# A list schedule that knows of the port between VectorE and GpSimd, and a fused alpha·x + bias

## The chip, the core and the metric

The kernel runs on one core of a Trainium2 chip. The metric is device microseconds of one execution; before the change the median of 3 runs is 1795.09 us (1792.98 to 1796.85). The engines' names in the profile: PE is TensorE (PEld its weight loads), DVE VectorE, ACT ScalarE, POOL GpSimd, SP the engine that issues the DMAs.

## What is computed

One inference step of a two-layer encoder (`DEPTH = 2`, width 1024), for 512 rows of a prompt and, beside it, 128 rows of samples (8 streams of 16 frames, with a cache of 1024 past frames each). Everything is fp32. Cut to what matters:

```python
for l in range(DEPTH):
    p = x @ w_in[l]
    y = [rms(y_A) | rms(y_B) | rms(y_C)] * g_mix[l]   # gMLP gating, latent attention, stick-breaking attention
    x = layer_norm(ALPHA * x + y @ w_out[l], ln1_g[l], ln1_b[l])
    h = square(relu(x @ w_up[l] + b_up[l])) @ w_down[l] + b_down[l]
    x = layer_norm(ALPHA * x + h, ln2_g[l], ln2_b[l])
```

The last line holds the term that the change touches: `ALPHA * x + b_down` is formed ahead, and the product with `w_down` is added to it.

## The kernel before

**Two lanes.** The prompt (`p_layer`, tiles t = 1 to 4 of 128 rows) and the samples (`s_layer`, tile t = 0) are two generators. `weave` lets them issue their instructions in turn. All rows live in one SBUF tile `xy` of 128 x 5 x 1024.

**fp32 by halves.** A matmul takes operands of a rounded type. So each fp32 operand is split in two: ScalarE copies it into the rounded type (`hi`), and then another engine subtracts that from the source (`lo`). Three matmuls (`mm3`, hi·hi, hi·lo, lo·hi) make one product. `split` (L577) does this; its subtraction goes to VectorE, except where the caller names GpSimd. VectorE does it for the weights (tiles w, wx, wS), for the hidden layer (hT) and for transposed activations out of PSUM (yT, pTs and others); GpSimd does it for the cached keys and values (cT, cN) and their rotary part (kr). The weights' and the cache's raw data, rawP, rawS, rawK and rawV, come by DMA into small rings.

**The stretch around the change, prompt.** `p_out_mlp` (L895) multiplies y with `w_out` in two halves of 512 columns, tile by tile. After the second half of tile t it calls `layer_norm` (L628): two bn_stats and a bn_aggr on VectorE give mv; `rstd_of` (L596) makes rs out of it in two instructions on GpSimd, a tensor_scalar and a power; two scalar_tensor_tensor on VectorE apply it, the first with mv and the gain, the second with rs and the bias. Gain, bias and `b_down` lie in tiles named hT, as they take slots of the ring that the hidden layer uses later. Then comes `x1(t - 1)` (L915): 8 transposes on TensorE of the tile before, with their splits, and in place on GpSimd the multiplication by ALPHA and the addition of `b_down`. The result is read again when the products with `w_down` are added, after the first four blocks of the hidden layer (`dve.tensor_tensor(xy, xy, pa, ADD)`, 128x512).

**The same for the samples.** `s_out_mlp` (L1686) does it for tile 0 alone (its two GpSimd instructions are L1715 and L1716); gain and bias lie in the ring rawS.

**What sets the order.** The generators do not issue into the engines' queues in their own order. Each instruction is noted in a `Plan` (`note`, L161) with its engine, a cost (`cost_of`, L365) and its dependencies. When all is noted, `ranks` gives each instruction a rank and `schedule` (L208) makes one list: it keeps a time at which each engine is free (`free`), takes the engine that can start first, and on it the instruction of the lowest rank among those that are ready by then. `issue` (L285) sets the instruction's start and end. `follow` (L358) fixes each engine's resulting order in the program, with no wait of its own: an instruction on the chip starts when its engine has come to it and its data are there. An instruction's `kind` is "copy" for `dve.tensor_copy` and empty otherwise; a "copy" starts when GpSimd is free, and GpSimd is free when it has ended. No `dve.tensor_copy` is called in the kernel. Nothing else in the list connects VectorE's time with GpSimd's. All instructions are issued by the helper at L403, so that the profile names them by tiles and not by lines.

Of the kernel before, what the change touches and what calls it, by code (L numbers as in the profile page):

```python
# [96 lines left out]
class Plan:  # L97

    AFTER = dict(pe=0.17, act=0.0, dve=0.0, pool=0.0, sp=0.0)
    HOP = dict(pe=0.055, act=0.035, dve=0.035, pool=0.08, sp=0.03)
    LAP = dict(pe=0.0, act=0.1, dve=0.08, pool=0.0, sp=0.0)

# [53 lines left out]
            self.masks[key] = r  # L158
        return self.masks[key]

    def note(self, eng, cost, ins, outs, srcs, kind="", nbytes=0):  # L161
        k = len(self.ops)
        deps = set()
        for ap, w in [(x, False) for x in srcs] + [(x, True) for x in outs]:
            t = self.tiles.get(ap.tensor.name)
            if t is None:
                continue
            m = self.region(ap)
            t["ops"].add(k)
            deps.update(o for o, x in t["writes"] if x & m)  # L170
            if t["tag"]["pool"]["psum"]:
                deps.add(t["bank"].get(eng, k))
                t["bank"][eng] = k
            if w:
                deps.update(o for o, x in t["reads"] if x & m or (t["tag"]["pool"]["psum"] and eng == "pe"))
                t["reads"] = [(o, x) for o, x in t["reads"] if x & ~m]
                t["writes"] = [(o, x) for o, x in t["writes"] if x & ~m] + [(k, m)]
            else:
                t["reads"].append((k, m))
        deps.discard(k)  # L180
        self.ops.append(dict(eng=eng, cost=cost, ins=ins, deps=deps, kind=kind, bytes=nbytes, then=[], by=self.now["by"], phase=self.now[self.now["by"]]))
        return k

    def glue(self, k0):
# [23 lines left out]
    def schedule(self, prio):  # L208
# [38 lines left out]
        end = [0.0] * n  # L247
        ready = [0.0] * n
        free = dict(pe=0.0, act=0.0, dve=0.0, pool=0.0, sp=0.0)
        dma = 0.0  # L250
        later = {e: [] for e in free}
        able = {e: [] for e in free}
        order = {e: [] for e in free}
# [29 lines left out]
                grant(t)  # L283

        def issue(k, e, s):  # L285
            nonlocal dma
            o = ops[k]
            if o["kind"] == "copy":
                s = max(s, free["pool"])
            if e == "sp":  # L290
                free[e] = s + 0.42
                dma = max(dma, s + 1.3) + o["bytes"] / 320e3
                f = dma + 0.45
            else:
                free[e] = s + o["cost"] - self.LAP[e]
                f = s + o["cost"] + self.AFTER[e]
                if o["kind"] == "copy":
                    free["pool"] = max(free["pool"], f)
            end[k] = f
            o["at"] = s  # L300
            order[e].append(k)
            for name in o["tiles"]:
                left[name] -= 1
                if not left[name]:
                    t = self.tiles[name]["tag"]
                    last = max(end[x] + 0.05 for x in self.tiles[name]["ops"])
                    t["slots"].append(last)
                    t["slots"].sort()
                    for x in opens.get(name, ()):
                        block[x] -= 1  # L310
                        floor[x] = max(floor.get(x, 0.0), last)
                        if not block[x]:
                            grant(self.tiles[x]["tag"])
                    grant(t)
            for x in succ[k]:
                hop = 0.0 if ops[x]["eng"] == e == "pe" else f + self.HOP[ops[x]["eng"]]
                ready[x] = max(ready[x], hop)
                need[x] -= 1
                if not need[x] and x not in glued:
                    loose(x)  # L320
# [7 lines left out]
        while done < n:  # L328
            best = None
            for e in free:  # L330
                if able[e]:
                    s = free[e]
                elif later[e]:
                    s = max(free[e], later[e][0][0])
                else:
                    continue
                if best is None or s < best[0]:
                    best = s, e
            if best is None:
                raise RuntimeError(f"no order: {n - done} left")  # L340
            s, e = best
            while later[e] and later[e][0][0] <= s:
                r, p, k = heapq.heappop(later[e])
                heapq.heappush(able[e], (p, k))
            p, k = heapq.heappop(able[e])
            while True:
                issue(k, e, s)
                done += 1
                if not ops[k]["then"] and not run:
                    break  # L350
                run = ops[k]["then"] + run
                k = run.pop(0)
                s = max(free[e], ready[k])
# [31 lines left out]
class Timed:  # L385
# [5 lines left out]
    def __getattr__(self, name):  # L391
        f = getattr(self.eng, name)

        def call(out, *a, **k):
            if name.startswith("preload"):
                r = f(out)
                self.pace.plan.note(self.key, 1.3, r.ins, [], [])
                return r
            ins = [x for n, x in [*enumerate(a), *k.items()] if isinstance(x, bass.AP) and n != "accum_out"]
            outs = [out] + ([k["accum_out"]] if "accum_out" in k else [])  # L400
            cost = cost_of(self.key, name, out, ins, "accum_out" in k)
            self.pace.add(self.key, cost, out.tensor.name, [x.tensor.name for x in ins])
            r = f(out, *a, **k)  # L403
            kind = "copy" if self.key == "dve" and name == "tensor_copy" else ""
            self.pace.plan.note(self.key, cost, r.ins, outs, ins, kind)
            return r
        return call


class Loads:  # L410
# [5 lines left out]
    def dma_start(self, out, src):  # L416
        self.pace.load(out.tensor.name, src.tensor.name, 4 * math.prod(out.shape))
        r = self.eng.dma_start(out, src)
        self.pace.plan.note("sp", 0.42, r.ins, [out], [src], "", 4 * math.prod(out.shape))
        return r  # L420


# [61 lines left out]
def hybrid_step(  # L484
# [410 lines left out]
    def p_out_mlp(l):  # L895
# [18 lines left out]

        def x1(t):  # L915
            transpose_x(xy[:, t], XT[:, 0, :, cols(t)], XT[:, 1, :, cols(t)], "acc")
            pool.tensor_scalar(xy[:, t], xy[:, t], ALPHA, 0.0, ALU.mult, ALU.add)
            pool.tensor_tensor(xy[:, t], xy[:, t], bd, ALU.add)

        l1 = 0.0  # L920
        for c in range(2):
# [764 lines left out]
    def s_out_mlp(l):  # L1686
# [25 lines left out]
        xT = so.tile([128, 2, 8, 128], F32R, tag="xS", name="x1TS")  # L1712
        yield at("sC", pace.t)
        transpose_x(xy[:, 0], xT[:, 0], xT[:, 1], "sC")
        pool.tensor_scalar(xy[:, 0], xy[:, 0], ALPHA, 0.0, ALU.mult, ALU.add)  # L1715
        pool.tensor_tensor(xy[:, 0], xy[:, 0], bcast(b_down[l], D), ALU.add)  # L1716
        yield at("x")
        down = [bank("x") for _ in range(2)]
        hts = []
# [47 lines left out]

    weave(nc, pace, thread(p_layer), thread(s_layer), RATE, now)
    order = pace.plan.schedule(pace.plan.ranks(*SPAN))
    print("PLAN span", pace.plan.span, "pe idle", pace.plan.idle)  # L1770
    pace.plan.follow(tc, order)


# [97 lines left out]
```

## Time and profile before

| what | value |
|---|---|
| median of 3 runs | 1795.09 us |
| the profiled execution, its own time | 1795.59 us |
| its span, first to last instruction | 1793.8 us |
| TensorE busy | 1683.3 us (94%) |
| VectorE busy | 1181.2 us (66%) |
| ScalarE busy | 994.7 us (55%) |
| GpSimd busy | 584.8 us (33%) |
| DMA queue of the loads and stores | 303.49 MB, 52.8% of 16 engines |
| granted TensorE clock, mean | 0.984 |

The first line is the kernel's time; the second is the one execution that the profile shows. The span leaves out what lies ahead of the first and after the last instruction. Busy time is the sum of an engine's instructions, with whatever each of them waited for after it had begun; a share is over the whole span, in which stretches with different limits follow each other. What the rows below show of waits is the idle time of an engine ahead of an instruction, put down to the engine and the tile that ended it.

### The profile page before, as it was taken

What the parts mean: (1) busy time and instruction counts of PE and PEld (TensorE: products, weight loads), DVE (VectorE), ACT (ScalarE), POOL (GpSimd) and SP (SyncE); (2) the same over time, 40 slices, a digit from 0 to 9 for tenths busy, and PEclk for the clock granted to TensorE, in tenths of its full rate; (3) what the DMA queues carried; (4) which work ended last, traced back from release to release, by engine and by line L of the source; (5) the groups of instructions that cost most, each with busy time, mean ns of one, the idle gap of its engine ahead of it and who ended that gap; (6) DMA issues with size and microseconds to landing.
All of it is one profiled execution on the core that took longest, in us unless ns stands there. A gap on an engine that the chain in (4) does not pass through costs nothing.

```text
span 1793.8 us, 24450 instructions
## 1 busy us (share of the span) xinstructions
PE 1683.3 (94%) x8756; PEld 1408.1 (78%) x8756; DVE 1181.2 (66%) x1582; ACT 994.7 (55%) x1739; POOL 584.8 (33%) x498
## 2 busy tenths in 40 slices
PE   8998999899999999999899989898999899999998
PEld 6888888677777778888688878787777677788886
DVE  3586685856676587666726766768566765876766
ACT  4575784545656556563226747745457555564631
POOL 0123455844564310000101324568446542100001
PEclk9999999999999999999999999999999999999999
DMA  6225566346445687674452356553465446875732
GB/s 248 92 70 169 192 173 213 117 141 203 152 134 160 178 280 239 199 249 130 151 154 71 101 156 192 173 196 118 151 201 156 139 143 190 269 245 187 254 127 91
DMA packets 145818, 305.06 MB, mean 170 GB/s; under 512 B 32032, under 2 KB 46496, under 8 KB 145696
## 3 DMA queue, kind: packets, MB, share of 16 engines
q1 hardware_dynamic: 145696, 303.49, 52.8%
q8 instruction: 69, 1.13, 0.3%
q14 instruction: 53, 0.43, 0.1%
HBM read 286.14 MB, written 17.30 MB: 169 GB/s over the span
## 4 chain that ended last, share of the span: by engine, by line
PE 56%; DVE 12%; DMA 10%; ACT 8%; POOL 7%; issue 6%; SPq 1%; POOLq 0%; ACTq 0%; DVEq 0%
PE acc L403 38%; PE sC L403 9%; PE x L403 8%; POOL rs L403 2%; POOL cN L403 2%; DVE xy L403 2%; DMA rawV<-in_t_ckvv_dram 2%; DVE a L403 2%; POOL cT L403 2%; DMA rawK<-in_t_ckv_dram 1%; DVE wx L403 1%; DMA rawP<-in_w_down_dram 1%; ACT w L403 1%; DVE z L403 1%; DVE w L403 1%
## 5 line engine op out<-in xcount | busy, mean ns | idle before, releaser
L403 PE MATMUL acc<-w,hT 128*128 128x512 f32 x1536 | 397.9, 397 | 4.1 <-ACT hT L403 3.6
L403 PE MATMUL acc<-yT,wx 128*128 128x512 f32 (+1 forms) x1632 | 399.2, 387 | 1.6 <-DVE wx L403 0.8
L403 PEld LDWEIGHTS acc<-yT,wx 128*128 128x128 f32 x1632 | 292.5, 191 | 59.7 <-DVE wx L403 1.7
L403 PEld LDWEIGHTS acc<-w,hT 128*128 128x128 f32 x1536 | 281.3, 188 | 66.5 <-ACT hT L403 6.0
L403 POOL TENSOR_TENSOR cT<-rawK,cT 128x512 fp32r<-128x512 f32 x128 | 187.9, 1475 | 192.5 <-ACT cT L403 167.3
L403 POOL TENSOR_TENSOR cN<-rawV,cN 128x512 fp32r<-128x512 f32 x128 | 189.8, 1488 | 154.1 <-ACT cN L403 152.3
L403 DVE TENSOR_TENSOR w<-rawP,w 128x1024 fp32r<-128x1024 f32 (+4 forms) x122 | 152.8, 1256 | 126.2 <-ACT w L403 124.4
L403 DVE TENSOR_TENSOR wS<-rawS,wS 128x1024 fp32r<-128x1024 f32 x144 | 179.2, 1249 | 81.2 <-ACT wS L403 80.4
L403 ACT CAST wS<-rawS 128x1024 fp32r<-128x1024 f32 x144 | 150.9, 1050 | 132.1 <-PE x L403 64.6
L403 PE MATMUL acc<-w,xT 128*128 128x512 f32 (+3 forms) x960 | 189.4, 353 | 5.1 <-DVE ev L403 2.5
L403 POOL TENSOR_SCALAR rs<-mv 128x1 f32<-128x1 f32 x20 | 22.1, 1105 | 522.9 <-DVE mv L403 521.8
L403 ACT CAST w<-rawP 128x1024 fp32r<-128x1024 f32 (+4 forms) x122 | 122.1, 1005 | 111.6 <-DMA rawP<-in_w_down_dram 53.7
L403 PEld LDWEIGHTS acc<-w,xT 128*128 128x128 f32 x960 | 160.9, 195 | 21.8 <-DVE ev L403 2.8
L403 DVE TENSOR_TENSOR xy<-xy,acc 128x512 f32<-128x512 f32 x128 | 87.2, 683 | 89.0 <-PE acc L403 88.6
L403 ACT CAST cN<-rawV 128x512 fp32r<-128x512 f32 x128 | 78.8, 620 | 80.8 <-DMA rawV<-in_t_ckvv_dram 28.3
L403 ACT CAST cT<-rawK 128x512 fp32r<-128x512 f32 x128 | 78.9, 619 | 56.7 <-DMA rawK<-in_t_ckv_dram 18.7
L403 DVE TENSOR_TENSOR wx<-rawP,wx 128x1024 fp32r<-128x1024 f32 x68 | 96.1, 1414 | 18.3 <-ACT wx L403 17.9
L403 PE MATMUL x<-cN,pTs 128*128 128x256 f32 x512 | 96.2, 294 | 12.5 <-POOL cN L403 6.9
L403 PEld LDWEIGHTS x<-cN,pTs 128*128 128x128 f32 x512 | 79.2, 192 | 34.0 <-POOL cN L403 16.2
L403 PE MATMUL sC<-wS,x1TS 128*128 128x512 f32 x384 | 99.5, 394 | 0.6 <-DVE wS L403 0.4
L403 PE MATMUL x<-wS,htS 128*128 128x512 f32 x384 | 99.5, 394 | 0.5 <-DVE htS L403 0.4
L403 PEld LDWEIGHTS x<-wS,htS 128*128 128x128 f32 x384 | 71.9, 188 | 17.9 <-DVE htS L403 0.8
(277 smaller groups left out, 2795.1 us busy)
## 6 DMA issues: line engine op xcount, KB each, us to landing
rawP<-in_t_wup_dram SPq DMA_DIRECT2D x64, 512.0 KB, 4.1
rawP<-in_w_down_dram SPq DMA_DIRECT2D x64, 512.0 KB, 4.1
rawS<-in_w_up_dram SPq DMA_DIRECT2D x64, 512.0 KB, 4.7
rawS<-in_w_down_dram SPq DMA_DIRECT2D x64, 512.0 KB, 4.3
rawK<-in_t_ckv_dram SPq DMA_DIRECT2D x64, 256.0 KB, 3.0
rawV<-in_t_ckvv_dram SPq DMA_DIRECT2D x64, 256.0 KB, 3.0
rawK<-in_t_sbk_dram SPq DMA_DIRECT2D x64, 256.0 KB, 2.8
rawV<-in_t_sbv_dram SPq DMA_DIRECT2D x64, 256.0 KB, 2.9
```

What stands on the lines that cost most here:

```text
L403: r = f(out, *a, **k)
```

## The change

It has two parts. In the list, an instruction carries a mark `shared` in place of `kind`. It is set on a VectorE instruction whose result and whose wide operands (64 elements or more in a partition) all lie outside PSUM, if it has more than one wide operand or is a tensor_copy. A marked instruction starts in the list when GpSimd is free, and a GpSimd instruction starts when the last marked one has ended. When VectorE is free, its next instruction is marked, and GpSimd stays busy for over 0.1 us more, the list looks at up to 8 ready instructions in the order of rank for one that is not marked, and takes that one if it ends by 0.4 us after GpSimd; otherwise it keeps the marked one, which then starts when GpSimd is free.

In the kernel, both x1 steps are one VectorE scalar_tensor_tensor in place of two GpSimd instructions.

```diff
-    def note(self, eng, cost, ins, outs, srcs, kind="", nbytes=0):
+    def note(self, eng, cost, ins, outs, srcs, shared=False, nbytes=0):
...
         def issue(k, e, s):
-            nonlocal dma
+            nonlocal dma, shared
             o = ops[k]
-            if o["kind"] == "copy":
+            if o["shared"]:
                 s = max(s, free["pool"])
+            if e == "pool":
+                s = max(s, shared)
...
-                if o["kind"] == "copy":
-                    free["pool"] = max(free["pool"], f)
+                if o["shared"]:
+                    shared = f
...
-                    s = free[e]
+                    s = max(free[e], shared) if e == "pool" else free[e]
...
             p, k = heapq.heappop(able[e])
+            if e == "dve" and ops[k]["shared"] and free["pool"] > s + 0.1:
+
+                aside = [(p, k)]
+                while able[e] and ops[aside[-1][1]]["shared"] and len(aside) < 8:
+                    aside.append(heapq.heappop(able[e]))
+                if ops[aside[-1][1]]["shared"] or s + ops[aside[-1][1]]["cost"] > free["pool"] + 0.4:
+                    k = aside.pop(0)[1]
+                else:
+                    k = aside.pop()[1]
+                for x in aside:
+                    heapq.heappush(able[e], x)
...
-            kind = "copy" if self.key == "dve" and name == "tensor_copy" else ""
-            self.pace.plan.note(self.key, cost, r.ins, outs, ins, kind)
+            wide = [x for x in ins if math.prod(x.shape[1:]) >= 64]
+            shared = self.key == "dve" and not any(x.space == PSUM for x in (out, *wide)) and (len(wide) > 1 or name == "tensor_copy")
+            self.pace.plan.note(self.key, cost, r.ins, outs, ins, shared)
...
         def x1(t):
             transpose_x(xy[:, t], XT[:, 0, :, cols(t)], XT[:, 1, :, cols(t)], "acc")
-            pool.tensor_scalar(xy[:, t], xy[:, t], ALPHA, 0.0, ALU.mult, ALU.add)
-            pool.tensor_tensor(xy[:, t], xy[:, t], bd, ALU.add)
+            dve.scalar_tensor_tensor(xy[:, t], xy[:, t], ALPHA, bd, ALU.mult, ALU.add)
...
-        pool.tensor_scalar(xy[:, 0], xy[:, 0], ALPHA, 0.0, ALU.mult, ALU.add)
-        pool.tensor_tensor(xy[:, 0], xy[:, 0], bcast(b_down[l], D), ALU.add)
+        dve.scalar_tensor_tensor(xy[:, 0], xy[:, 0], ALPHA, bcast(b_down[l], D), ALU.mult, ALU.add)
```

## Rows read from the trace of the kernel before

**Rows 1.** The page: the span, and each engine's busy time with its share.

```profile
span 1793.8 us, 24450 instructions
PE 1683.3 (94%) x8756; PEld 1408.1 (78%) x8756; DVE 1181.2 (66%) x1582; ACT 994.7 (55%) x1739; POOL 584.8 (33%) x498
```

**Rows 2.** TensorE's waits: for whom, us in total, times, longest us.

```profile
PE acc L403 <- DVE xy L403: 9.6, 6, 2.7
...
PE sC L403 <- DVE o L403: 7.5, 7, 3.3
PE x L403 <- POOL cN L403: 6.9, 12, 1.8
...
PE x L403 <- DVE z L403: 4.0, 2, 3.1
PE sC L403 <- POOL cT L403: 3.7, 5, 1.3
PE acc L403 <- ACT hT L403: 3.6, 4, 1.2
...
PE acc L403 <- DVE nm L403: 3.4, 1, 3.4
...
PE x L403 <- POOL cT L403: 2.2, 4, 0.9
...
PE sC L403 <- POOL kr L403: 1.3, 2, 0.7
```

**Rows 3.** Stretches: length, busy PE, PEld, DVE, ACT, POOL, granted clock, DMA, GB/s.

```profile
1222.90:1226.40 3.50, 3.50 (x19) 3.37 (x18) 3.50 (x7) 2.05 (x5) 3.42 (x3) 0.51 0.62 178
...
342.30:345.70 3.40, 3.40 (x16) 3.12 (x15) 2.15 (x2) 1.91 (x3) 2.70 (x3) 0.50 0.58 177
...
499.30:502.70 3.40, 3.40 (x10) 2.64 (x9) 3.40 (x3) 1.14 (x2) 3.40 (x2) 0.50 0.75 227
311.00:351.00 40.00, 31.68 (x197) 27.98 (x197) 33.34 (x36) 19.74 (x34) 37.28 (x26) 0.96 0.39 119
1203.00:1243.00 40.00, 33.03 (x197) 28.65 (x196) 32.74 (x37) 19.16 (x32) 34.80 (x24) 0.96 0.37 114
```

**Rows 4.** Timeline from 1214 to 1223: start, length, engine, operation, [idle before].

```profile
1214.63 1.03 POOL L403 TENSOR_SCALAR rs<-mv 128x1 f32<-128x1 f32 x1
...
1215.74 2.41 POOL L403 TENSOR_TENSOR xy<-xy,hT 128x1024 f32<-128x1024 f32 x1
...
1216.73 2.50 DVE L403 TENSOR_TENSOR wx<-rawP,wx 128x1024 fp32r<-128x1024 f32 x1
...
1218.11 1.54 POOL L403 TENSOR_TENSOR rs<-rs,mhalf 128x1 f32<-128x1 f32 x1
...
1219.68 2.27 DVE L403 SCALAR_TENSOR_TENSOR xy<-xy,rs,hT 128x1024 f32<-128x1024 f32 x1 [0.45 <-POOL rs L403]
...
1222.10 0.41 PE L403 MATMUL acc<-identr,xy 128*128 128x128 f32 x2 [2.48 <-DVE xy L403]
```

**Rows 5.** By tile: count, duration in ns (min/median/max), first and last start.

```profile
L403 POOL TENSOR_SCALAR xy<-xy x10: 1047/1066/1817, 312.5 to 1543.6; 128x1024 f32<-128x1024 f32 x10
...
L403 DVE SCALAR_TENSOR_TENSOR xy<-xy,mv,hT x8: 1273/1286/2150, 301.9 to 1226.8; 128x1024 f32<-128x1024 f32 x8
L403 DVE SCALAR_TENSOR_TENSOR xy<-xy,rs,hT x8: 1271/2277/3425, 303.9 to 1232.8; 128x1024 f32<-128x1024 f32 x8
...
L403 POOL TENSOR_TENSOR xy<-xy,hT x8: 2390/2410/3327, 314.7 to 1244.5; 128x1024 f32<-128x1024 f32 x8
...
L403 DVE TENSOR_TENSOR relu<-relu x64: 672/687/1808, 350.3 to 1763.6; 128x512 f32<-128x512 f32 x64
...
L403 DVE TENSOR_TENSOR wx<-rawP,wx x68: 1167/1225/3359, 268.3 to 1753.7; 128x1024 fp32r<-128x1024 f32 x68
...
L403 POOL TENSOR_TENSOR cN<-rawV,cN x128: 1257/1296/3510, 194.2 to 1501.1; 128x512 fp32r<-128x512 f32 x128
...
L403 DVE TENSOR_SCALAR o<-o,lr x8: 347/354/830, 289.5 to 1305.5; 128x256 f32<-128x256 f32 x8
```

More of the change, by code (lines that the diff above doesn't have):

```diff
@@ L180, in note @@
         deps.discard(k)
-        self.ops.append(dict(eng=eng, cost=cost, ins=ins, deps=deps, kind=kind, bytes=nbytes, then=[], by=self.now["by"], phase=self.now[self.now["by"]]))
+        self.ops.append(dict(eng=eng, cost=cost, ins=ins, deps=deps, shared=shared, bytes=nbytes, then=[], by=self.now["by"], phase=self.now[self.now["by"]]))
         return k
@@ L249, in schedule @@
         free = dict(pe=0.0, act=0.0, dve=0.0, pool=0.0, sp=0.0)
-        dma = 0.0
+        dma = shared = 0.0
         later = {e: [] for e in free}
@@ L418, in dma_start @@
         r = self.eng.dma_start(out, src)
-        self.pace.plan.note("sp", 0.42, r.ins, [out], [src], "", 4 * math.prod(out.shape))
+        self.pace.plan.note("sp", 0.42, r.ins, [out], [src], False, 4 * math.prod(out.shape))
         return r
@@ L1769, in hybrid_step @@
     order = pace.plan.schedule(pace.plan.ranks(*SPAN))
-    print("PLAN span", pace.plan.span, "pe idle", pace.plan.idle)
     pace.plan.follow(tc, order)
```

## The prediction

> **What bounds the kernel now.** I read the page first. TensorE is busy 1683.3 of 1793.8 us, so no rearrangement can win more than its 110.5 us of idle time and what a lowered clock costs; VectorE (66%) and GpSimd (33%) have room on average [rows 1]. A change to these two engines can matter only where TensorE waits for them, so the waits of TensorE came second. 9.6 us of them end with the tile xy on VectorE and 3.4 with nm, 14.1 with the splits cN, cT and kr on GpSimd (6.9, 3.7, 2.2, 1.3), 4.0 with z, 3.6 with hT [rows 2]. Third, the busy times by stretch: in the two stretches of 40 us in which the prompt's x1 runs, TensorE is idle for 8.3 and 7.0 us, while VectorE is busy for 33.3 and 32.7 us and GpSimd for 37.3 and 34.8 [rows 3]. There the supporting engines are the limit.
>
> Fourth, the timeline of one such tile shows why. GpSimd does the first step of rs at 1214.63, then 2.41 us of x1's addition, and the second step of rs only at 1218.11. Meanwhile the wx split on VectorE takes 2.50 us and ends when 1.1 us have passed since GpSimd's addition ended; the second step of rs takes 1.54 us and ends just after wx does. VectorE's last pass of the layer norm then takes 2.27 us, and TensorE, which has to transpose its result, has stood for 2.48 us at 1222.10 [rows 4]. So a VectorE instruction with two operands in SBUF and a GpSimd instruction do not run side by side: whichever is second waits for the first. The durations say the same for all instances: relu has a median of 687 ns and a maximum of 1808, wx 1225 and 3359, the GpSimd split cN 1296 and 3510; the last pass of the layer norm, which usually starts beside x1's addition, has a minimum of 1271 and a median of 2277 [rows 5]. The list schedule knows of none of this: `kind` is "copy" for tensor_copy alone, which the kernel never calls, so its times overlap what the chip puts in series.
>
> **The change, part by part.**
>
> (A) *x1 moves to VectorE.* Removed from GpSimd: 10 multiplications of 1.07 us and 10 additions of 2.41 (8 in the rows; I take the sample's two at the same length), 34.8 us [rows 5]. Added to VectorE: 10 scalar_tensor_tensor of 128x1024 with all tensors in SBUF. The same kind and size exists: 1.273 us at least, 1.286 in the median, 2.150 at most with a wait in it [rows 5]; I take 1.29, together 12.9. No DMA and no step of another engine moves. What waits for x1's result is the addition of the down projection, later by a whole group of up projections, so the result is late for nobody; the tile's old readers, the transposes, are the same, and the slot of b_down, which an hT tile takes over, comes free no later, as 3.48 us of GpSimd become 1.29 of VectorE. Behind x1 on VectorE stand the splits of the same transposes, which need a ScalarE copy of them first, so x1 brings no later wait into the queue.
>
> On the path: each tile's chain (statistics, two steps of rs on GpSimd, two passes on VectorE, transposes) loses what x1 put into it. In the tile shown the second step of rs can start 2.4 us earlier, and the last pass shrinks from 2.27 towards 1.27; 3.4 us against a stall of 2.48, so this stall can go entirely [rows 4, 5]. The waits of this kind are 9.6 + 3.4 = 13.0 us [rows 2]; nm's one wait I count with xy's, since a VectorE instruction as short as nm keeps TensorE for 3.4 us only if a long one stood ahead of it. Bounds 0 and 13.0. I take 10, since other splits on GpSimd still come between the steps. With them goes part of the clock: two of the stalls are followed by a stretch of 3.4 to 3.5 us at a granted clock of 0.50 and 0.51 of 2.4 GHz, thus 1.2 GHz, in which TensorE is busy throughout [rows 3]; each costs half its length, 1.7 us. Bounds 0 and 3.4; I take 2.0. Gain 12.0.
>
> Against it: x1(t-1) can now stand on VectorE ahead of the norm of the next tile, in 3 tiles of each layer: 6 times 1.29 is 7.7 us at most, 0 at least. TensorE has other work in most of that time; I take 1.3, one instance.
>
> (B) *The list keeps the two engines apart.* No wait is added to the program; only the order on each queue changes, and the times by which TensorE's order is made. In the list a marked VectorE instruction now starts after GpSimd's, a GpSimd instruction after a marked one, and where GpSimd is busy VectorE takes an instruction that is not marked, such as a split out of PSUM, if it ends by 0.4 us after GpSimd. TensorE's order then asks for cN, cT, kr, z and hT nearer to when they really come. At stake: 14.1 + 4.0 + 3.6 = 21.7 us [rows 2], and one more stretch at half clock after a stall on cN, 1.7 us [rows 3]. Bounds: 21.7 + 1.7 = 23.4 gained, or, with all of it shifted elsewhere, nothing; the loss is the third rival. I take a third of the waits, 7, because two thirds have other causes in the chain (the ScalarE copy ahead, the landing of a load), and 1 of the clock. Gain 8.0. For new stalls that a reordered list brings I take 2.0 off, one stall of the size seen at 1222.10 [rows 4].
>
> I leave the 7.5 us that TensorE waits for o [rows 2] out of B, although o's tensor_scalar is stretched as well, from 354 to 830 ns [rows 5]: the change marks only instructions with two wide operands. The Trainium skill, SBUF — State Buffer, section "Who interferes with whom", says that tensor_scalar in a two-port mode holds the pair that GpSimd needs, too; the trace agrees by that 830. By that rule the list still has a blind spot; had the change marked tensor_scalar, a third of 7.5 would add 2.5 us to the gain.
>
> The sample's x1 (two instances) lies where GpSimd has nothing else; I cost it at 0, and at 2 x 1.29 if VectorE were late there.
>
> **Sum**, against the profiled execution's 1795.6 (span 1793.8 plus 1.8 around it): 1795.6 - 12.0 + 1.3 - 8.0 + 2.0 = 1778.9. The median of the three runs is 0.5 lower, so the forecast is 1778.4, given as 1778. All gains and no cost would be 13.0 + 3.4 + 23.4 = 39.8, thus 1755; no gain and all of x1's cost 1803.
>
> **Rivals.**
>
> 1. *Only x1 pays.* The lock is the chip's, and an order alone separates nothing: what GpSimd and VectorE each have to do stays, and the stalls of B turn up at other tiles. For: no wait is added. Against: the waits on cN and cT are short (6.9 us over 12 waits), which a small shift covers. Time: 1795.1 - 12.0 + 1.3 = 1784.4, between 1781 and 1793.
>
> 2. *The list is changed, and nothing comes of it.* The norm's chain stays late for another reason: with x1 gone, the next split cN or cT takes its place between the two steps of rs (cN 1.296 us in the median [rows 5]), and the last pass is stretched by that one; what A keeps, B gives back in new stalls. For: cN alone is 128 such splits, so that one is often queued when a step of rs comes. Time: 1795, within 3.6 us.
>
> 3. *Slower: VectorE lets the wrong instruction pass.* The list sends an unmarked instruction ahead of a marked one of higher rank, up to 0.4 us beyond GpSimd's end. The marked ones are what the prompt's matmuls need: 68 of wx and 64 of relu alone [rows 5], 132 x 0.4 = 53 us of lateness at most. TensorE follows its fixed order, so where nothing is queued ahead of the late one it stands. The net gain of A is 10.7: from one uncovered in five this decides, and at one in three, 17.6 us, with nothing from B, the time is 1795.1 - 10.7 + 17.6 = 1802. For: TensorE has already waits on hT, whose relu was stretched. Against: hT's 3.6 us is the only wait for the prompt's operands among the longer ones [rows 2], so most of them are ready ahead of time.
>
> **How the numbers follow.** The forecast has 0.50, with its own range of 1765 to 1788; rival 1 has 0.22, rival 2 0.11, rival 3 0.17. 0.2% is 3.6 us, about what a measurement of this kernel can tell from no change. Faster by more than that: the forecast and most of rival 1 (0.20), 0.70. Within it: rival 2 and the rest of rival 1, 0.13. Slower: rival 3, 0.17. The range goes from 1762, below which the gains would have to be nearly all of the bounds, to 1799, which takes in rivals 1 and 2 and the near part of rival 3.
>
> **What would show it.** Right for A: no GpSimd instruction writes xy any more; ten VectorE scalar_tensor_tensor on xy with hT or rawS at about 1.29 us; the last pass of the norm has a median under 1.7 us, and TensorE's waits for xy and nm together are under 4 us. Right for B: maxima of relu, wx and cN stay, but their means come down, since fewer meet; the waits of TensorE for cN, cT and kr fall from 14.1 to about 9. TensorE's busy time stays, less what the clock gives back, and its idle time falls from 110 to about 95. Wrong, if the idle time stays at 110 with the waits under new names (rival 2), or if waits for wx, w and hT on VectorE grow by 10 us or more (rival 3).

## The result, and the profile after

The changed kernel takes 1804.33 us in the median of 5 runs, against 1795.09 us: ratio 1.0053 (95% interval 1.0035 to 1.0072), slower by half a per cent. One of the five, at 5753 us, was disturbed and does not enter the ratio. A second set of runs on another chip gave 1.0033 (1.0019 to 1.0048). The prediction was 1778 us, in a range from 1762 to 1799, so it was wrong, and on the wrong side.

The page of the profiled execution (1802.48 us, mean granted clock 0.972 where before had 0.984), its span and busy times, against [rows 1]:

```profile
span 1800.6 us, 24422 instructions
PE 1689.7 (94%) x8756; PEld 1421.8 (79%) x8756; DVE 1179.1 (65%) x1592; ACT 994.7 (55%) x1739; POOL 560.7 (31%) x478
```

TensorE's idle time is what it was: 1800.6 - 1689.7 = 110.9 us, before 110.5. The span grew by 6.8 us, and 6.4 of them are TensorE's own busy time, for the same 8756 matmuls, at a lower mean clock: more of them ran at 1.2 GHz. In a second profiled execution of the same kernel (`r5_after_again`, span 1794.9) TensorE is busy for 1684.7 us and idle for 110.2, so the idle time is the steadier of the two findings. TensorE's waits after (columns as in [rows 2]):

```profile
PE sC L417 <- ACT gh L417: 17.8, 2, 9.2
...
PE x L417 <- DVE z L417: 7.3, 6, 2.4
PE acc L417 <- DVE xy L417: 4.4, 7, 1.6
...
PE sC L417 <- ACT cT L417: 3.8, 2, 3.6
PE sC L417 <- POOL cT L417: 3.3, 5, 1.8
...
PE x L417 <- ACT wS L417: 2.9, 1, 2.9
PE x L417 <- ACT cT L417: 2.8, 2, 1.5
PE x L417 <- POOL cN L417: 2.0, 3, 0.9
...
PE sC L417 <- ACT wS L417: 1.9, 1, 1.9
...
PE sC L417 <- POOL kr L417: 1.1, 1, 1.1
...
PE acc L417 <- DVE nm L417: 0.4, 1, 0.4
...
PE x L417 <- POOL cT L417: 0.2, 1, 0.2
```

The waits that the change was aimed at did shrink: xy and nm from 13.0 to 4.8 us, GpSimd's cN, cT and kr from 14.1 to 6.6. The same time is back under other names: z 7.3 (4.0 before), ScalarE's cT 6.6 (2.0), its wS 4.8 (0.3), and above all gh with 17.8 us in two waits of 8.5 and 9.2. gh is the operand of the prompt's spatial gating, in the mixing stage that opens each layer. In the kernel before, TensorE waited 3.4 us for it in all:

```profile
PE sC L403 <- DVE gh L403: 2.4, 2, 1.2
...
PE sC L403 <- ACT gh L403: 1.0, 2, 0.5
```

Where in the kernel this falls is shown by stretches (columns as in [rows 3]). First the kernel before: the mixing stage of each layer (up to the last product of the prompt's input projections), then the feed-forward stage of each (its eight groups of four hidden slices, from the end of the output products on):

```profile
0.00:156.50 156.50, 143.04 (x840) 129.53 (x841) 92.25 (x150) 89.74 (x180) 35.58 (x60) 0.99 0.43 145
889.00:1046.20 157.20, 143.38 (x855) 130.26 (x853) 93.73 (x154) 83.31 (x174) 32.66 (x50) 0.96 0.39 121
327.00:889.00 562.00, 541.15 (x2548) 438.42 (x2549) 376.77 (x420) 302.15 (x459) 170.49 (x120) 0.99 0.57 181
1219.60:1785.10 565.50, 542.15 (x2544) 435.47 (x2543) 378.45 (x418) 299.98 (x455) 167.09 (x117) 0.99 0.56 178
```

Then the same four stretches after, and the two stretches at the lower clock around the waits for gh:

```profile
0.00:160.90 160.90, 142.51 (x840) 130.52 (x841) 93.17 (x150) 90.16 (x180) 31.37 (x60) 0.97 0.42 142
888.50:1055.60 167.10, 144.93 (x855) 132.40 (x853) 94.33 (x153) 83.75 (x174) 29.75 (x50) 0.92 0.38 114
333.70:888.50 554.80, 537.30 (x2540) 435.11 (x2539) 376.37 (x422) 300.79 (x457) 166.69 (x112) 0.99 0.58 183
1228.10:1791.90 563.80, 542.80 (x2533) 440.44 (x2531) 376.11 (x421) 297.28 (x452) 153.49 (x106) 0.98 0.55 176
142.00:152.20 10.20, 6.98 (x29) 6.98 (x30) 7.30 (x17) 3.21 (x7) 2.31 (x6) 0.50 0.34 113
1036.30:1049.90 13.60, 5.75 (x23) 5.57 (x24) 8.76 (x19) 4.12 (x10) 4.53 (x9) 0.50 0.35 121
```

The two mixing stages went from 313.7 to 328.0 us (+14.3), the two feed-forward stages from 1127.5 to 1118.6 (-8.9), and the rest (attention, output products and the end) from 352.6 to 354.0 (+1.4). The sum is the span's +6.8. In the second execution the same three are 328.2, 1112.2 and 354.5 us: the mixing stages lose the same, the feed-forward stages gain 15.3. So the change gained where it was meant to, less than I had forecast, and lost as much or more in a stage that I had not looked at.

How gh came late shows in the timeline of the first mixing stage. Before:

```profile
136.51 1.65 POOL L403 TENSOR_TENSOR gst<-gst,mhalf 128x8 f32<-128x8 f32 x1
...
138.19 0.69 DVE L403 TENSOR_TENSOR gvt<-gvt,gst 128x512 f32<-128x512 f32 x1 [1.82 <-POOL gst L403]
...
138.97 0.62 ACT L403 CAST gh<-gvt 128x512 fp32r<-128x512 f32 x1 [0.38 <-DVE gvt L403]
...
139.90 0.22 PE L403 MATMUL sC<-gh,wsT 128*128 128x128 f32 x1
```

After:

```profile
136.19 0.20 POOL L417 TENSOR_SCALAR gst<-gst 128x8 f32<-128x8 f32 x1 [4.39 <-DVE gst L417]
...
138.40 1.06 POOL L417 TENSOR_TENSOR rs<-rs,mhalf 128x1 f32<-128x1 f32 x2
...
139.43 1.65 POOL L417 TENSOR_TENSOR gst<-gst,mhalf 128x8 f32<-128x8 f32 x1
...
139.90 2.38 DVE L417 TENSOR_TENSOR wq<-rawS,wq 128x768 fp32r<-128x768 f32 x3
...
142.19 0.68 DVE L417 TENSOR_TENSOR gvt<-gvt,gst 128x512 f32<-128x512 f32 x1
...
144.14 0.51 ACT L417 CAST wq<-rawS 128x384 fp32r<-128x384 f32 x1 [2.86 <-DMA rawS<-in_w_uq_dram]
144.56 0.61 ACT L417 CAST gh<-gvt 128x512 fp32r<-128x512 f32 x1
...
145.22 0.47 PE L417 MATMUL sC<-gh,wsT 128*128 128x128 f32 x1 [8.52 <-ACT gh L417]
```

The chain of gh is four short steps on three engines. Before, GpSimd's power on gst ends at 138.16 and TensorE starts 1.74 us later. After, the power comes 2.9 us later in GpSimd's queue, behind rs; VectorE's multiplication stands behind three marked splits of wq; and ScalarE's copy stands behind a copy that waits for a load until 144.14. From the tensor_scalar of gst on, these places cost 3.0, 1.1 and 1.7 us. In the second layer the power ends at 1038.01 and the multiplication starts only at 1041.31. None of the chain's instructions became slower in the stretch shown. Their places in the three queues changed, each by a little, and TensorE, whose own order is fixed, stood for 8.52 us. From 142.0 on, within the wait, the granted clock was 0.50 (1.2 GHz), and it stayed there until 152.2. The stretch of the second layer begins 7.0 us before its wait ends. In both together TensorE worked for 12.7 us at that clock.

The durations that answer to [rows 5]:

```profile
L417 DVE SCALAR_TENSOR_TENSOR xy<-xy,rs,hT x8: 1265/1706/2412, 313.1 to 1239.5; 128x1024 f32<-128x1024 f32 x8
L417 DVE SCALAR_TENSOR_TENSOR xy<-xy,hT x8: 1211/1284/2152, 322.6 to 1247.9; 128x1024 f32<-128x1024 f32 x8
...
L417 DVE TENSOR_SCALAR o<-o,lr x8: 347/354/1382, 278.6 to 1307.8; 128x256 f32<-128x256 f32 x8
```

### The profile page after: what moved, and what is told of

Its sections match the earlier page's. It is cut to its first block, busy times and chain, and to the rows that moved or that the text cites. A ratio compares the mean times of both kernels' runs of the same rounds, so it can differ in the third digit from the quotient of the medians.

```text
span 1800.6 us, 24422 instructions
## 1 busy us (share of the span) xinstructions
PE 1689.7 (94%) x8756; PEld 1421.8 (79%) x8756; DVE 1179.1 (65%) x1592; ACT 994.7 (55%) x1739; POOL 560.7 (31%) x478
## 5 line engine op out<-in xcount | busy, mean ns | idle before, releaser
L417 POOL TENSOR_TENSOR cT<-rawK,cT 128x512 fp32r<-128x512 f32 x128 | 201.1, 1578 | 178.7 <-ACT cT L417 157.1
L417 POOL TENSOR_TENSOR cN<-rawV,cN 128x512 fp32r<-128x512 f32 x128 | 194.3, 1524 | 167.7 <-ACT cN L417 160.9
L417 DVE TENSOR_TENSOR wS<-rawS,wS 128x1024 fp32r<-128x1024 f32 x144 | 175.2, 1223 | 78.9 <-ACT wS L417 78.7
L417 PEld LDWEIGHTS x<-cN,pTs 128*128 128x128 f32 x512 | 82.1, 194 | 31.0 <-ACT cN L417 10.2
L417 DVE TENSOR_TENSOR wx<-rawP,wx 128x1024 fp32r<-128x1024 f32 x68 | 90.6, 1332 | 12.1 <-ACT wx L417 11.6
```

## The experiments

18 runs followed, one of them of the kernel after itself; each ratio is to runs of the kernel before on the same chip. The theories, as the expectations number them: **T1**, the marks make gh late in the mixing stage, and that is the loss; **T2**, the step that lets unmarked instructions pass marked ones makes the prompt's operands late (rival 3 of the prediction); **T3**, the fused x1 on VectorE is what costs; **T4**, any edit of the list re-deals the order, and the time scatters by half a per cent; **T5**, x1 itself costs time on VectorE under a marked list (T3 once more); **T6**, the list gives VectorE the first claim where the chip does not (**T7**: it is not that); **T8**, what counts is where the sample's work stands beside the prompt's.

### The two parts, each alone

`e1_x1_alone`: the list of before, both x1 fused on VectorE. `e2_list_alone`: the list of after, both x1 as two GpSimd instructions:

```diff
-            dve.scalar_tensor_tensor(xy[:, t], xy[:, t], ALPHA, bd, ALU.mult, ALU.add)
+            pool.tensor_scalar(xy[:, t], xy[:, t], ALPHA, 0.0, ALU.mult, ALU.add)
+            pool.tensor_tensor(xy[:, t], xy[:, t], bd, ALU.add)
```

> The list of before (no marks), and only the two x1 steps as one VectorE instruction each. Theory T1 (the loss comes from the marks in the list alone: in the spatial gating of each layer GpSimd's power for gst is put behind a run of marked weight splits): x1 by itself is a gain, the waits of TensorE for xy and nm fall from 13.0 us to under 6, and the time is 1783 to 1792. Rival T3 (the fused x1 on VectorE is what costs): 1800 or more. Rival T2 (VectorE lets unmarked instructions pass marked ones, so w, wx and hT come late): says nothing against T1 here, 1783 to 1792.

> The list of after with its marks, x1 on GpSimd as before. T1: TensorE's two long waits for gh (8.5 and 9.25 us in after) stay, and what x1 gained is gone: 1804 to 1816. T2: the same. T3: near before or under it, 1797 or less.

x1 alone: 1791.42 us, ratio 0.9989 (0.9973 to 1.0004), no difference that can be told; that is T1's time and rules out T3 in this list, though xy and nm fell to 7.9 us and not under 6. The list alone: 1779.29, ratio 0.9912 (0.9889 to 0.9936), faster, where T1 and T2 had 1804 or more and only T3 1797 or less, though its mixing stages are as long as after's (162.9 + 165.7 = 328.6 us) and it has 17.3 us of waits for gh. It wins in the feed-forward stages:

```profile
335.90:885.00 549.10, 535.34 (x2536) 434.49 (x2535) 374.75 (x418) 300.59 (x457) 174.93 (x122) 0.99 0.57 186
1226.90:1772.90 546.00, 534.01 (x2527) 434.87 (x2525) 367.13 (x416) 297.00 (x450) 162.26 (x114) 0.99 0.55 183
```

1095.1 us, where before has 1127.5 and after 1118.6. So T1 names a real loss, but not what tells the kernel after from a faster one: with x1 fused as well, the feed-forward stages lose 23.5 us (17.1 by the second execution). The parts do not add: -0.1% and -0.9% give +0.3 to +0.5%.

One reason shows in the list alone. Its x1 is still on GpSimd, and TensorE waits for xy as little as in the kernel after, and for nm not at all:

```profile
PE acc L417 <- DVE xy L417: 4.9, 7, 2.1
```

So here the marks had taken 8.1 of the 13.0 us that the fused x1 was to win, and beside them it had 0.1 left. That is so in `r6_list_not_mix` and `r8_list_03` too (4.6 and 5.8 us), but not in every marked list with x1 on GpSimd (11.4 in r17 and 18.0 in r14, below).

### The mixing stage without marks

`e3_not_mix` (after) and `r6_list_not_mix` (the list alone) mark nothing while the prompt mixes:

```diff
-            shared = self.key == "dve" and not any(...)
+            shared = self.key == "dve" and not self.pace.plan.now["P"].startswith("mix") and not any(...)
```

> After, but an instruction noted while the prompt is in its mix stage carries no mark, so the list of the spatial gating is made as before. T1: the two long waits for gh go (17.8 us in after, 3.4 in before), and with them about 19 us by which the end of that stage was later than in before (6 in the first layer, 12 to 13 in the second): 1778 to 1790. T2 and T3: those causes lie outside the mix stage, so little changes, 1798 to 1808.

> The marked list without the fused x1, and without marks in the mix stage. Theory T1' (the marks cost 14 to 19 us in the mix stages, as two long waits for gh and the half clock after them, and gain elsewhere): the list alone had 1779 with both waits in it, so this has 1760 to 1770, with the waits for gh under 4 us. Rival T4 (every change of the list reshuffles thousands of instructions, and the time scatters by some 10 us whichever cause is taken away): the waits for gh go, and the time still lies between 1770 and 1790.

1785.27 us (0.9949, 0.9928 to 0.9969) and 1772.1 (0.9883, 0.9862 to 0.9904): 0.8 to 1.0% and 0.3% under their pairs with marks throughout, the second within both intervals. The waits for gh in `e3_not_mix`:

```profile
PE sC L417 <- DVE gh L417: 1.6, 2, 0.9
PE sC L417 <- ACT gh L417: 1.0, 2, 0.5
```

and its two mixing stages take 157.1 + 161.4 = 318.5 us. This effect is the one that held in every run: over all kernels profiled, the two mixing stages take 321 to 335 us in the 12 executions with marks in them (two of the kernel after) and 311 to 319 in the 8 without, with no overlap. T1 holds for the place and for the price there: 14.3 us against before, 9.5 against `e3_not_mix`.

### Passing, and the first claim

`e4_no_aside` leaves out the block that lets an unmarked VectorE instruction pass. `r11_after_turn` takes the first claim from VectorE when the list chooses the next engine:

```diff
-                    s = max(free[e], shared) if e == "pool" else free[e]
+                    s = free[e]
```

> After without the block that takes an unmarked instruction ahead of a marked one; marked ones and GpSimd still exclude each other. T1: the two long waits for gh stay within 2 us of 17.8 together, and the time stays at 1798 to 1810. T2: the block is the cause, so the time falls to 1795 or less. T3: 1800 to 1810, unchanged.

> The kernel after, but when the list decides which engine is next, GpSimd is no longer set back to the end of VectorE's last marked instruction (the instruction's own start still is). T6 (the list gives VectorE the first claim on the lock, so GpSimd's short steps of the spatial gating are ordered late, while the chip lets the two engines alternate): TensorE's waits for gh fall from 17.8 us to under 8, and the time is 1780 to 1792 us. Rival T7 (the choice of the next engine is not it; VectorE's marked splits stand ahead of the gating's multiplication on VectorE in any such list): gh stays at 14 to 18 us and the time at 1796 to 1806.

Without passing 1790.69 us (0.9979, 0.9958 to 1.0), with gh at 16.0 us: the loss at gh does not come from passing. The time is T2's (1795 or less) and not T1's; whether that is the passing itself stays open, as this list also moved the sample's work, which turns out to matter below. With GpSimd's turn 1792.66 (0.999, 0.9975 to 1.0006), and gh falls, but not under 8, so that neither T6's numbers nor T7's came:

```profile
PE sC L417 <- ACT gh L417: 11.5, 2, 6.5
```

T6 accounts for a third of gh's lateness; where the rest comes from (the marks' own start times, or ScalarE's queue) was not tried.

### How far does a meaningless edit move it?

`r5_after_again` is the kernel after once more; `r7_after_03` and `r8_list_03` change the tolerance of the passing step from 0.4 to 0.3 us, in the kernel after and in the list alone:

```diff
-                if ops[aside[-1][1]]["shared"] or s + ops[aside[-1][1]]["cost"] > free["pool"] + 0.4:
+                if ops[aside[-1][1]]["shared"] or s + ops[aside[-1][1]]["cost"] > free["pool"] + 0.3:
```

> After once more, unchanged, beside before on the chip of this call, since the list alone came out at a ratio of 0.991 and x1 alone at 0.999, while both together had 1.005 on another chip. If the parts do not add up: 1.003 to 1.007 again. If the first measurement was off: 0.995 or less.

> After with one constant of the list changed that means nothing: an instruction taken ahead may end 0.3 us after GpSimd and not 0.4. T4: the time moves by 5 us or more from after's, to either side. Rival T5 (the fused x1 itself costs some 20 us under a marked list): it stays within 4 us of after's.

> The marked list without the fused x1 (1779 before), with the same meaningless change from 0.4 to 0.3 us. T4: it moves by 5 us or more from 1779, to either side. T5: it stays within 4 us of 1779.

1799.17 us (1.0033, 1.0019 to 1.0048), 1812.03 (1.0106, 1.0089 to 1.0124) and 1783.71 (0.995, 0.9931 to 0.9969). A tenth of a microsecond in one comparison of the list makes the kernel after 0.5 to 0.7% slower and the list alone 0.4% slower (4.4 us, between the two forecasts; its interval and that of `e2_list_alone` just meet). That is T4's scatter, as large as the effect under study.

### Is it x1 itself?

From the kernel after: the prompt's eight x1 fused and the sample's two on GpSimd (`r9_fused_prompt`), the complement (`r10_fused_sample`), and all ten fused but not marked (`r12_x1_unmarked`, a line behind each x1):

```diff
+            pace.plan.ops[-1]["shared"] = False
```

> The kernel after with the sample's two x1 put back on GpSimd (multiplication and addition); the prompt's eight stay on VectorE. The list of marks alone, with all ten on GpSimd, gave 1779 to 1784 us, all ten on VectorE 1799 to 1804. T5 (the prompt's eight cost it: each is a marked instruction of 1.3 us that stands on VectorE ahead of splits and of the norm in the mlp stage): 1794 to 1804 us, and TensorE's waits for VectorE's z and ScalarE's cT and wS in the mlp stages stay as in the kernel after (7.3, 6.6 and 4.8 us). T5' (the sample's two cost it, as each stands ahead of the sample's own chain): 1776 to 1788 us. T4 (neither by itself; any edit of the list scatters by about 0.5%): anywhere from 1780 to 1804, and this kernel and the one with the sample's fused alone need not add up to the kernel after.

> The complement: the sample's two x1 on VectorE, the prompt's eight back on GpSimd, the list with marks. T5 (the prompt's eight cost it): 1774 to 1786 us. T5' (the sample's two cost it): 1794 to 1804 us. T4: anywhere from 1776 to 1804; it is borne out if the two differences from the list of marks alone do not add up to the one of all ten (about 20 us) within 8 us.

> The kernel after, but the ten x1 on VectorE are not marked, so that the list takes them for instructions that can run beside GpSimd's and may send them ahead of marked ones while GpSimd is busy. On the chip they meet GpSimd's as before. T5'' (x1 costs something through its mark, since a marked x1 holds GpSimd's splits back in the list): 1776 to 1790 us. Rival (it is x1's 1.3 us on VectorE, or the scatter of the list): 1795 to 1810 us.

1795.91 us (1.0004, 0.9985 to 1.0024), 1790.26 (0.9961, 0.9944 to 0.9979) and 1793.51 (0.9996, 0.998 to 1.0013). Against the list alone the prompt's eight cost 0.9% and the sample's two 0.5%: they add up to the 1.2 to 1.4% of all ten, as T5 has it and T4 does not. But TensorE's wait for z, which T5 had staying at 7.3 us, is 0.2 in the first; the second kernel's time lies in neither of its two narrow ranges, and the third's between its two. And ten instructions of 1.28 us are 12.8 us in all, the prompt's eight stand within 20 us of the start of each layer's feed-forward stage, and much of the time was lost 100 to 300 us behind them. In the orders of TensorE's matmuls I found a difference: in the list alone the sample's up and down projections begin beside the prompt's sixth group of hidden slices in both layers, in the kernel after only in the first, and in the second beside the fifth. That gave T8.

### The sample's place

The list ranks a prompt instruction by the share of its layer's TensorE work that is done, and a sample instruction by the share of its own work, stretched over the interval `SPAN` of the prompt's layer. A later interval puts the sample behind:

```diff
-SPAN = 0.25, 0.93
+SPAN = 0.28, 0.93
```

That is `r13_after_span` (after), `r16_not_mix_span` (on `e3_not_mix`), `r17_list_not_mix_span` (on `r6_list_not_mix`, x1 on GpSimd) and `r18_before_span28` (before). `r14_list_span` has (0.22, 0.93) on the list alone, `r15_before_span` (0.28, 0.96) on before.

> The kernel after with one constant changed, SPAN from (0.25, 0.93) to (0.28, 0.93): the sample's instructions get later ranks beside the prompt's. By the order that comes out, the sample's up and down projections then run beside the prompt's sixth group of four feed-forward slices (96 matmuls of the down projection) in both layers, where in the kernel after they do so in the first layer only, and begin one group earlier in the second; the list of marks alone has them there in both. T8 (what the fused x1 costs under the marked list is this position of the sample, about 0.65% per layer: stalls of both chains where they share groups one to five, none in group six): 1785 to 1795 us, with TensorE idle in the five groups of the second layer down from 21 to about 12 us. T5 (it is x1 on VectorE itself): 1797 to 1806.

> The list of marks alone (x1 on GpSimd) with SPAN (0.22, 0.93): the sample's instructions get earlier ranks, so that its up and down projections lie beside groups one to five in both layers, as in the kernel before. T8 (the position of the sample is what made the list alone quicker than the kernel before and the kernel after): 1795 to 1810 us. T5 (x1's place is what counts, and it is on GpSimd here): 1776 to 1788.

> The kernel before with SPAN (0.28, 0.96) and nothing else: no marks, x1 on GpSimd, but the sample's up and down projections pushed to groups six to eight. T8 in its strong form (the position alone pays, marks or not): 1772 to 1787 us. T8 in its weak form (without marks the list's order stalls at GpSimd's splits wherever the sample stands): 1788 to 1800.

> The kernel after with no marks while the prompt is in its mixing stage (1785 us in the earlier run) and SPAN (0.28, 0.93): x1 fused on VectorE, the sample beside group six in both layers, no waits for gh. T8: 1766 to 1778 us, as the same list with x1 on GpSimd (1772). T5: 1781 to 1790.

> The best list so far (marks, none while the prompt mixes, SPAN (0.28, 0.93); 1769 us with x1 fused on VectorE) with x1 back on GpSimd. If the fused x1 costs nothing by itself once the sample stands later: within 5 us of 1769, thus 1764 to 1774. If it pays what the prediction's part A gave it (10.7 us net): 1776 to 1784. If it still costs what it did in the first twelve runs (0.7 to 1.4%): 1744 to 1757.

> The kernel before with SPAN (0.28, 0.93) and nothing else, the same constant as in the two quick kernels. If later ranks of the sample pay only under marks: 1789 to 1798 us. If they pay in any list: 1775 to 1787, and the marks would then be worth less than the comparison of the kernels with SPAN (0.28, 0.93) and the kernel before makes them seem.

| kernel | us | ratio to before (95%) |
|---|---|---|
| r13: after, sample later | 1783.82 | 0.994 (0.9916 to 0.9964) |
| r14: list alone, sample earlier | 1803.08 | 1.0049 (1.0028 to 1.0069) |
| r15: before, sample later | 1795.3 | 1.0014 (0.9994 to 1.0035) |
| r16: after, no marks in mixing, sample later | 1769.27 | 0.9861 (0.9839 to 0.9882) |
| r17: the same, x1 on GpSimd | 1780.79 | 0.9931 (0.9914 to 0.9949) |
| r18: before, sample later | 1804.06 | 1.0052 (1.0033 to 1.0071) |

r13, r14 and r16 met T8's numbers or beat them: both kernels with the fused x1 became 0.9 to 1.1% faster, the list alone with the sample earlier 1.4% slower. r15 came out in T8's weak form: without marks the later place gained nothing. So T5 falls as the cause: with x1 on VectorE the kernel reaches 1769 us, the lowest median of all, 1.4% under before. But r13's idle time in the first five groups of the second layer's feed-forward went from 21 to 17 us and not to 12. And with the later ranks r17 became 0.5% slower than the same list without them (0.9883 to 0.9931), r18 0.5% slower than before.

I took these two for the end of T8, but the traces say that neither tests it. The rows show the sample's up projections (192 matmuls a layer, tile x1TS) that TensorE does while the prompt's fifth group of the second layer runs: stretch, length, busy PE (count), clock, DMA, GB/s, in the kernel after, the list alone, r17 and r18:

```profile
1499.20:1583.20 84.00, 11.73 (x48) 0.98 0.74 239
...
1477.50:1545.30 67.80, 0.16 (x1) 1.00 0.66 213
...
1470.50:1534.30 63.80, 0.00 (x0) 1.00 0.60 183
...
1496.20:1582.30 86.10, 12.19 (x48) 0.98 0.68 215
```

In r17 the sample stood clear of group five before the edit too (`r6_list_not_mix`), and in r18 it never left it. Counted like this in both layers, T8's order holds in every list with marks, though neighbouring intervals overlap:

| sample's up projections in group five | marks throughout | no marks in mixing | no marks |
|---|---|---|---|
| in neither layer | 0.9912 to 0.9979 (e2, r13, r8, r10, e4) | 0.9861 to 0.9931 (r16, r6, r17) | 1.0014 (r15) |
| in one layer | 0.9996 to 1.0053 (r12, r9, after) | 0.9949 (e3) | no run |
| in both layers | 0.999 to 1.0106 (r11, r14, r7) | no run | 0.9989 to 1.0052 (e1, before, r18) |

(r9 has 48 of them there in the first layer and 19 in the second.) The tenth of a microsecond of r7 was not without meaning either: it moved the sample into group five in the first layer as well, where r8 left it in place. Why sharing group five is dearer is not shown, and within one cell the time still differs by 0.6 to 1.2%.

r16 and r17 are worth reading side by side, as they differ by x1 alone. x1 on GpSimd first (r17), then fused (r16):

```profile
PE acc L417 <- DVE xy L417: 11.4, 6, 4.4
```

```profile
PE acc L417 <- DVE xy L417: 2.6, 2, 2.0
```

and the longest of these waits in r17's timeline:

```profile
1215.20 3.31 POOL L417 TENSOR_TENSOR xy<-xy,hT 128x1024 f32<-128x1024 f32 x1
1216.24 3.35 DVE L417 SCALAR_TENSOR_TENSOR xy<-xy,rs,hT 128x1024 f32<-128x1024 f32 x1
...
1219.65 0.69 PE L417 MATMUL acc<-identr,xy 128*128 128x128 f32 x2 [4.36 <-DVE xy L417]
```

That is the stall of part A as the prediction described it: the norm's last pass beside x1's addition, 3.35 us for one that takes 1.27 alone, and TensorE behind it. In r16 it is gone, and the kernel is 11.5 us faster (0.7%); r17's time lies in the range that its expectation gave for part A. It is one pair, measured on two chips, and no larger than what other edits moved.

What one edit was worth, then, in each list that it was made in:

| the edit | in which list | change of the ratio |
|---|---|---|
| x1 fused | of before | -0.1% |
| | marks | +1.2 to +1.4% |
| | marks, tolerance 0.3 | +1.6% |
| | marks, none in mixing | +0.7% |
| | marks, none in mixing, sample later | -0.7% |
| sample later (0.28) | of before | +0.5% |
| | marks and x1 fused | -0.9 to -1.1% |
| | the same, none in mixing | -0.9% |
| | marks, none in mixing, x1 on GpSimd | +0.5% |

Where the fused x1 cost 0.7 to 1.6%, it came with the sample in group five, in one layer more (marks; none in mixing) or in both (tolerance 0.3). With the sample in the same place it is worth -0.1% in the list of before, -0.7% in r16 against r17, -0.2% in r16 against r6 and +0.3% in r13 against e2, the last two within what the intervals allow.

## Why the prediction was wrong

**The bound and its reading were right, as far as one pair shows.** The wait on the norm's last pass exists, and in r17 it is x1 on GpSimd that makes it (11.4 us, against 2.6 in r16).

**(A), gain 12.0 less 1.3.** Its signs came, two of them just short: GpSimd writes xy no more; the ten x1 on VectorE take 1.284 us in the median of the prompt's eight, against 1.29; xy and nm fell from 13.0 to 4.8 us (I had said under 4); the last pass has a median of 1.706 (I had said under 1.7). At the one pair where the waits of before are there and the sample stands in the same place, the worth of A is 11.5 us against 10.7. In the list of before it is 2 us (1795.3 x 0.0011), not to be told from nothing, and in three lists with marks it comes with a loss of 12 to 28.

**(B), gain 8.0 less 2.0.** Alone the list gained 0.9%, 16 us, with the new stalls in it: more than I gave it. But the marked lists that left the sample where before has it (r11, r14, r7) are no faster than before, so the gain came with the sample's move, and not only with the waits that I priced. cN, cT and kr fell to 6.6 us in the kernel after, further than the 9 that I forecast, but only to 11.5 in the list alone. That the engines would meet less often came half true: VectorE's means fell (relu 897 to 848 ns, wx 1414 to 1332), GpSimd's rose (cN 1488 to 1524, cT 1475 to 1578).

**The step that failed first** is the last term of (B): "For new stalls that a reordered list brings I take 2.0 off, one stall of the size seen at 1222.10". The mixing stages alone brought 14.3 us: two stalls of 8.5 and 9.2 us where 3.4 in all stood before, and 10.2 and 13.6 us at half clock around their ends. I had sized the term by a stall in the stage that the change aims at, and never asked where else in the kernel marked VectorE instructions and a GpSimd step of a chain stand together. That question has an answer in the trace of before: the chain of gst, gvt and gh runs over GpSimd, VectorE and ScalarE among marked splits of wq.

**The sum failed with it.** I added A and B as if each kept its worth beside the other. They aim at the same waits: with the marks alone xy and nm stood at 4.9 us, with both at 4.8, so the 10 us that I gave A on them were nearly all taken already. Outside the mixing stages I expected 18.7 us and found 7.5 (8.9 - 1.4) in one execution and 13.4 (15.3 - 1.9) in the other. And with x1 fused the list kept the sample in group five of the second layer, out of which the marks alone had moved it. Moving it out (r13) is worth 0.9 to 1.1%, leaving the marks out of the mixing stages (e3) 0.8 to 1.0%; with both (r16) the kernel takes 1769 us, 9 less than the forecast. What stays open is why group five is the dearer place, and why the later place gained nothing without marks (r15).

**The rivals.** Rival 2's sign came: "the idle time stays at 110 with the waits under new names". Its time of 1795 left out that TensorE itself would be busy for longer, by 6.4 us in the first execution and 1.4 in the second. Rival 3 had the time (1802) by another mechanism: waits for w, wx and hT were 0.5, 1.1 and 2.1 us, where its sign asked for 10 more, and leaving out the passing did not remove gh. The range ended at 1799 and so held only the near part of rival 3.

**The blind spot that I named** is there: o's tensor_scalar, unmarked, went from a mean of 503 to 594 ns and a maximum of 1382. By the Trainium skill, SBUF — State Buffer, section "Who interferes with whom", tensor_scalar in a two-port mode holds the pair that GpSimd needs, too; the trace after agrees, by that maximum: it ran beside a split of cN and ended 0.15 us after it.

## What to carry to other kernels

Where one greedy list orders all engines, an edit of its rules or of one instruction re-deals the whole order: price it by a few edits that should mean nothing (here they moved the time by 0.4 to 0.7%), look in the trace for what else they moved, and do not add up the worths of parts that aim at the same waits. A rule that delays one engine is to be looked at where that engine holds a short step in a long chain, not only where the rule is wanted; here, leaving the marks out of one stage took the new stall away in all four lists that were tried. A stall is paid twice if the clock falls with it, so read the granted clock of the stretch around each new wait.

## What the runs showed of the hardware

Where both had work, the two engines took turns. The list gives VectorE's marked instructions the first claim; on the chip, after:

```profile
1386.62 3.76 POOL L417 TENSOR_TENSOR cT<-rawK,cT 128x512 fp32r<-128x512 f32 x2
...
1386.95 2.30 DVE L417 TENSOR_TENSOR wx<-rawP,wx 128x1024 fp32r<-128x1024 f32 x1
...
1389.29 0.69 DVE L417 TENSOR_TENSOR z<-x,tmp 64x512 f32<-64x512 f32 x1
...
1390.12 0.48 PE L417 MATMUL x<-cT,qS 128*128 128x512 f32 x1 [2.43 <-DVE z L417]
```

wx, 1.22 us in its median, takes 2.30 beside two splits of cT, which take 3.76 together where two alone take some 2.6 by the median of cN, a split of the same size. z, which reads one operand from PSUM, takes 0.67 to 0.69 us in all of its 32 instances; it is late because it stands behind wx in VectorE's queue, and TensorE waits for it. Apart from that, the same kernel moves by up to 1.1% from execution to execution, and mostly with the granted clock: `e4_no_aside` ran between 1778.5 us at a mean clock of 0.980 and 1798.4 at 0.974 on one chip. The first of these is its profiled execution, so its stages are those of a quick one.
